# Retention in three bursts, and its read-out turned by VectorE and a trip to DRAM instead of TensorE

## The chip, the cores and the metric

The kernel runs on one core of one Trainium2 chip. The metric is the time of the device in microseconds (us) for one execution, lower is better. The engines of a core have short names in the profile: PE is TensorE's matmul, PEld its weight load, DVE is VectorE, ACT is ScalarE, POOL is GpSimd, SP is SyncE, which here only sends DMA transfers.

## The reference

A trunk of two layers on a sequence of 512 tokens and 1024 channels. Each layer normalizes its input, projects it, runs three mixers side by side (RWKV-7, retention and a spatial gating unit, SGU), merges them by sigmoid gates, projects back, and ends with a gated feed-forward part. The change touches retention (4 heads, q and k of 64, v of 128 channels, chunks of 128 tokens) and the merge:

```python
def retention_branch(p, cos, sin):
    q, k, v, g = jnp.split(p, [RET_QK_WIDTH, 2 * RET_QK_WIDTH, 2 * RET_QK_WIDTH + RET_V_WIDTH], axis=-1)
    q = rotary(q, cos, sin); k = rotary(k, cos, sin) * (RET_QK_DIM ** -0.5)
    ...
    scores = jnp.einsum('bhnid,bhnjd->bhnij', qc, kc) * decay_in[:, None]
    inner = jnp.einsum('bhnij,bhnje->bhnie', scores, vc)
    kv = jnp.einsum('bhnjd,bhnje,hj->nbhde', kc, vc, k_dec)
    _, R_prev = lax.scan(lambda R, kv_n: (R * chunk_decay + kv_n, R), zeros, kv)
    cross = jnp.einsum('bhnid,nbhde,hi->bhnie', qc, R_prev, q_dec)
    y = inner + cross
    y = y * lax.rsqrt(jnp.mean(y * y, axis=-1, keepdims=True) + EPS)
    return y.reshape(B, S, RET_V_WIDTH) * jax.nn.silu(g)
# merge: for each branch, y (512 channels) @ W_branch -> 1024 channels, times sigmoid(gate), summed over branches
```

The einsums are cut here to their core; the batch is 1.

## The kernel before

**Matrix products.** Activations lie with channels on the partitions and the 512 tokens along the free axis. Every float32 product of a weight and an activation is made of three: both are split into a high part and the rest (hi and lo of an activation, sh and sl, or wh and wl, of a weight), and PE adds lo x sh, hi x sh and hi x sl into one PSUM tile `acc` (line L153). A product over 512 channels is so 4 x 3 = 12 matmuls of 128x512; I call them by their number.

**The way of a weight.** SP loads 256 KB of raw weight into a tile `wr` (L123); there are NRAW = 3 of these. ScalarE casts it to `sh` (L136), VectorE takes the difference `sl` (L137), and with that the raw tile is free for the next load. Casts stand some products ahead of their use in the order (AHEAD, three or more). All engines run their own instructions in the order written, which a scheduler has fixed when the program is built; within it the kernel keeps some orders by hand.

**Order in the mixer.** The string SEQ sets the order of the second half of a layer's mixer: S is one call of retention (`ret_row`), H loads q and k of retention (`ret_heads`: qF, kF from DRAM, qS and vs copied to the other half of the partitions by ScalarE's queue), G is one of the four SGU pieces (`sgu_out`: 4 matmuls, then hi and lo of `sgm`), U a part of the SGU projection, Y the read-out of retention (`ret_out`), and 0, 2 and 1 are one merge each (`merge`) of RWKV, SGU and retention. Eight merges of each branch make a layer.

**Retention** runs in five calls: each reads out the chunk before (scores x v and state R x q into the tiles X), makes the scores of the next, and the first two make the states R. After a read-out ScalarE squares it by heads (`rsq`, sums in `rss`), VectorE multiplies it with the silu gate into `vt` (called yg in the code), GpSimd makes `rrr`, the inverse root of the mean, and ScalarE scales each head's 128x128 block. The result has tokens on the partitions; `ret_out` turns it with 16 PE transposes a layer (L959) and splits it from PSUM into hi and lo.

**A merge** takes a tile `gth`, which GpSimd's queue fills with the gates from DRAM (L1021), makes the 12 matmuls, and lets VectorE form (gate + 1) x product (L1024). SGU's result is added by GpSimd, retention's by VectorE (L1027), and the sum is split by ScalarE and VectorE (L145, L146) for the projection back.

Of the kernel before, what the change touches and what calls it, by code (L numbers as in the profile page):

```python
# [17 lines left out]
S = 512  # L18
NC = 4
# [2 lines left out]
RWC, RETC, SGC = 1792, 1536, 1024  # L22
NU, NR, NFP = 31, 16, 39
FILL = (35, 2, 1)
SEQ = "0 H 0 0 G G S U S U G S 0 G S 0 0 S 2 2 0 0 Y 2 2 1 2 1 2 1 2 1 2 1 1 1 1"
NRAW = 3
START = "z0 w0 z1 w1 z2 w2 z3 s0 z4 s1 w3 z5 s2 s3 w4 z6 s4 w5 z7 s5 s6 w6 s7 w7"
AHEAD = {None: 2, "p": 4, "r": 3, "f": 3, "u": 5}
# [21 lines left out]
class Emit:  # L50
# [312 lines left out]
    def mixer(self, l, nst):  # L363
        self.pool = None
        with self.tc.tile_pool(name=f"rw{l}", bufs=1) as rp:
            self.rwp = rp
            self.filler = self.fillers(l)
            st = self.rwkv(l, nst)
        self.fill(99, True)
        self.rp = self.tc.tile_pool(name=f"ff{l}", bufs=NFP)  # L370
        self.fp = self.rp.__enter__()
        self.gup = self.f(n="gup")
        with self.tc.high_priority():
            self.nc.sync.dma_start(self.gup, self.a["gup"][l])
        self.pool = "f"
        sg, out = self.sgu_v(l), self.rwkv_out(l, *st)
        self.wsp = self.split(self.ws.rearrange("p g i -> p (g i)"), self.f)
        for step in (sg, sg, out, sg, None, out, sg, out, out):
            next(step) if step else self.sgu_bias()
        yrw, ysg, mg, out, m2 = self.yrw, [], [], [], 0  # L380
        self.pool = "r"
        rest = self.sgu_u(l, range(2, 4))
        rows = iter([(None, 0), (0, 1), (1, 2), (2, 3), (3, None)])
        for step in SEQ.split():
            if step == "S":
                self.ret_row(*next(rows))
            elif step == "G":
                ysg.append(self.sgu_out(len(ysg)))
            elif step == "H":
                self.ret_heads()  # L390
            elif step == "U":
                next(rest), next(rest)
            elif step == "Y":
                yret = self.ret_out()
            elif step == "0":
                mg.append(self.merge(l, 0, len(mg), yrw))
            elif step == "2":
                mg[m2] = self.merge(l, 2, m2, ysg, mg[m2])
# [468 lines left out]
    def ret_heads(self):  # L867

        A, V, T, po = self.nc.scalar, self.nc.vector, self.nc.tensor, self.tc.keep_in_program_order
        self.qF, self.kF = [], []  # L870
        for j in range(4):
            t = self.r((128, 4, 128), n="qF" if j < 2 else "kF")
            self.nc.sync.dma_start(t.rearrange("p c t -> p (c t)"), self.qk[128 * j:128 * j + 128, :])
            (self.qF if j < 2 else self.kF).append(t)
        self.qS, Rt = self.r(n="qS"), [self.f((128, 2, 2, 128), n="R") for _ in range(4)]
        for h in range(2):
            self.nc.scalar.dma_start(self.qS[64 * h:64 * h + 64], self.qF[1][64 - 64 * h:128 - 64 * h].rearrange("p c t -> p (c t)"))
        self.Rs, vs = [None] + [Rt[n // 2][:, n % 2] for n in range(7)], [self.f((128, 2, 2, 128), n="vs") for _ in range(2)]
        self.vs = [vs[c // 2][:, c % 2] for c in range(NC)]
        for c in range(NC):  # L880
            for h in range(2):
                self.nc.scalar.dma_start(self.vs[c][64 * h:64 * h + 64], self.heads(self.vt[c], h)[64 - 64 * h:128 - 64 * h])
# [20 lines left out]
            else:  # L903
                V.tensor_tensor(self.Rs[n + 1], self.Rs[n], at(n), op=ADD)

    def ret_row(self, read, score):


        nc, V, A, T, po = self.nc, self.nc.vector, self.nc.scalar, self.nc.tensor, self.tc.keep_in_program_order
        hv = [slice(0, 64), slice(64, 128)]  # L910
        X, new = [self.sm((128, 4, 128)) for _ in range(2)], [[True, True], [True, True]]
        hd = [(j, p, h) for j in range(2) for p in range(2) for h in range(2)]

        def mm(b, q, o, lhsT, rhs, stop=True):
            po(T.matmul(o, lhsT, rhs, start=new[b][q], stop=stop, skip_group_check=True))  # L915
            new[b][q] = False

        if read is not None:
            v, g = self.vt[read], self.yg[read]
            for j, p, h in [(j, p, 1 - h) for j, p, h in hd]:  # L920
                i, o = 2 * j + h, h ^ j
                w = v[hv[p], 128 * i:128 * i + 128] if p == o else self.vs[read][hv[o], j, :]
                mm(o, p, X[o][hv[p], j, :], self.sc[hv[o], h, p, :], w, read == p == 0)
            for j, p, h in hd:
                if read or p:
                    o, ts = h ^ j, slice(128 * read + 64 * p, 128 * read + 64 * p + 64)
                    q = self.qS if j else self.qF[0].rearrange("p c t -> p (c t)")
                    mm(o, p, X[o][hv[p], j, :], q[hv[o], ts], self.Rs[2 * read + p][hv[o], j, :])
        if score is not None:
            for j, p, h in hd:  # L930
                ts = slice(64 * p, 64 * p + 64)
                mm(h, h ^ j, X[h][hv[h ^ j], 2, ts], self.kF[j][hv[h], score, ts], self.qF[j][hv[h], score, ts])
        if read is not None:
            sq, ss = self.u((128, 4, 128), n="rsq"), self.small((128, 4), "rss")
            for i in range(4):
                A.activation(sq[:, i, :], X[i % 2 ^ i // 2][:, i // 2, :], AF.Square, accum_out=ss[:, i:i + 1])
            for o in range(2):
                V.tensor_tensor(self.heads(g, o), X[o][:, 0:2, :], self.heads(g, o), op=MUL)
        if score is not None:
            sc = self.u((128, 2, 2, 64), n="sc")  # L940
            for h in range(2):
                V.tensor_tensor(sc[:, h], X[h][:, 2, :].rearrange("q (p t) -> q p t", t=64), self.c("le64").unsqueeze(1).to_broadcast([128, 2, 64]), op=MUL)
            self.sc = sc
            if score < 2:
                self.ret_states(4 * score, 4 + 3 * score)
        if read is not None:
            V.tensor_scalar(ss, ss, 4.0 / 128, 4e-6, op0=MUL, op1=ADD)
            rr = self.small((128, 4), "rrr")
            nc.gpsimd.tensor_tensor(rr, ss, self.c("mhalf")[:, 0:4], op=POW)
            for i in range(4):  # L950
                o = g[:, 128 * i:128 * i + 128]
                A.activation(o, o, AF.Copy, scale=rr[:, i:i + 1])

    def ret_out(self):
        out = []
        for h in range(4):
            pt = self.sm()
            for c in range(NC):
                self.tc.keep_in_program_order(self.nc.tensor.transpose(pt[:, c * 128:c * 128 + 128], self.yg[c][:, h * 128:h * 128 + 128], self.c("ident")))  # L959
            out.append(self.split(pt, self.f))  # L960
        return out


# [53 lines left out]
    def merge(self, l, br, m, y, sum=None, add=None):  # L1017

        nc = self.nc
        t = self.f(n="gth")  # L1020
        nc.gpsimd.dma_start(t, self.gd[br, m])  # L1021
# [279 lines left out]
```

## Time and profile before

| | |
|---|---|
| median of 3 runs | 1703.14 us (1702.77 to 1706.36) |
| the profiled execution's own time | 1702.28 us |
| its span, first to last instruction | 1700.6 us |
| mean granted TensorE clock | 0.999 |
| busy: PE, PEld | 1692.3 us (100%), 1390.6 us (82%) |
| busy: DVE, ACT, POOL | 1141.6 (67%), 765.9 (45%), 245.4 us (14%) |
| largest groups: the three matmuls of L153 with `sh` | 432.3, 431.6, 431.1 us, 1108 each |

Busy shares are of the span. A row of the timeline gives the start in us from the span's begin, the length, engine, line, operation and output<-inputs with the number of records; in brackets stands how long the engine sat idle before it and what ended that. A row of a table of groups ends in "busy us, mean ns of one | idle us of the engine before them, and what ended it". In a table of stretches each engine has its busy us, then come PE's clock, the busy share of the DMA engines and GB/s. A 128x128 float32 matmul can leave two records.

### The profile page before, as it was taken

Reading aid. Unit: us, or ns where it says so; the run is one execution under the profiler, and the core shown is the slowest. Engines: PE = TensorE matmul, PEld = TensorE weight load, DVE = VectorE, ACT = ScalarE, POOL = GpSimd, SP = SyncE. Lnnn points to the kernel's source line nnn. Section 1 sums busy time; section 2 is a strip of 40 time slices with the busy share of each in tenths; the row PEclk is TensorE's granted clock in tenths of the full one; section 3 lists DMA queues with packets and bytes.
Section 4 is the critical chain, followed back from the end, with each engine's and each line's share of the span. In section 5 each row is a group of like instructions: output and inputs, shape, how many; then the busy total and the mean of one; then the engine's idle time right before and its main releaser. Section 6 shows DMA issues by size and latency. Waiting matters only on the chain.

```text
span 1700.6 us, 28356 instructions
## 1 busy us (share of the span) xinstructions
PE 1692.3 (100%) x10564; PEld 1390.6 (82%) x10564; DVE 1141.6 (67%) x2032; ACT 765.9 (45%) x1341; POOL 245.4 (14%) x326
## 2 busy tenths in 40 slices
PE   9999999999999999999999999999999999999998
PEld 7888877888888888888888888778888888888887
DVE  7887856567569777653367786564765798876432
ACT  7564433535355444333255634345343554443322
POOL 1122235114100000000011203441141000000010
PEclk9999999999999999999999999999999999999999
DMA  5334566446443333243332346555364454432531
GB/s 175 91 101 151 147 151 152 141 130 194 137 149 100 96 97 99 69 119 110 115 113 80 112 142 155 148 141 161 108 210 141 132 138 123 124 107 68 155 100 55
DMA packets 151337, 214.20 MB, mean 126 GB/s; under 512 B 48416, under 2 KB 57248, under 8 KB 151200
## 3 DMA queue, kind: packets, MB, share of 16 engines
q1 hardware_dynamic: 129552, 171.62, 34.2%
q0 software_dynamic: 9600, 21.77, 4.9%
q10 hardware_dynamic: 12048, 19.00, 3.4%
q8 instruction: 83, 1.36, 0.3%
q14 instruction: 54, 0.44, 0.1%
HBM read 181.92 MB, written 23.07 MB: 121 GB/s over the span
## 4 chain that ended last, share of the span: by engine, by line
PE 99%; DMA 0%; ACT 0%; DVE 0%; issue 0%
PE acc L153 88%; PE sm L153 4%; PE sm L647 2%; PE acc L287 1%; PE sm L561 1%; PE sm L915 1%; PE acc L1009 0%; PE sm L524 0%; PE sm L523 0%; DMA g<-pcols 0%; PE sm L898 0%; PE sm L959 0%; PE sm L805 0%; PE sm L795 0%; PE sm L578 0%; PE sm L579 0%
## 5 line engine op out<-in xcount | busy, mean ns | idle before, releaser
L153 PE MATMUL acc<-lo,sh 128*128 128x512 f32 x1108 | 432.3, 390 | 0.0
L153 PE MATMUL acc<-hi,sh 128*128 128x512 f32 x1108 | 431.6, 390 | 0.0
L153 PE MATMUL acc<-hi,sl 128*128 128x512 f32 x1108 | 431.1, 389 | 0.0
L136 ACT CAST sh<-wr 128x512 fp32r<-128x512 f32 (+1 forms) x385 | 235.1, 615 | 380.2 <-PE acc L153 263.4
L137 DVE TENSOR_TENSOR sl<-wr,sh 128x512 fp32r<-128x512 f32 (+1 forms) x385 | 263.4, 687 | 170.5 <-ACT sh L136 104.8
L153 PEld LDWEIGHTS acc<-lo,sh 128*128 128x128 f32 x1108 | 208.0, 188 | 44.1 <-issue 0.7
L153 PEld LDWEIGHTS acc<-hi,sl 128*128 128x128 f32 x1108 | 208.0, 188 | 43.7 <-issue 0.3
L153 PEld LDWEIGHTS acc<-hi,sh 128*128 128x128 f32 x1108 | 208.0, 188 | 42.9 <-issue 0.2
L136 ACT CAST wh<-wr 128x512 fp32r<-128x512 f32 x194 | 120.2, 620 | 227.9 <-PE acc L153 209.2
L153 PE MATMUL acc<-lo,wh 128*128 128x512 f32 x556 | 219.4, 395 | 0.0
L153 PE MATMUL acc<-hi,wl 128*128 128x512 f32 x556 | 217.0, 390 | 0.0
L153 PE MATMUL acc<-hi,wh 128*128 128x512 f32 x556 | 216.6, 390 | 0.0
L137 DVE TENSOR_TENSOR wl<-wr,wh 128x512 fp32r<-128x512 f32 x195 | 138.9, 712 | 111.6 <-ACT wh L136 104.7
L153 PEld LDWEIGHTS acc<-hi,wl 128*128 128x128 f32 x556 | 104.4, 188 | 22.6 <-issue 0.7
L153 PEld LDWEIGHTS acc<-lo,wh 128*128 128x128 f32 x556 | 104.3, 188 | 22.6 <-issue 0.3
L153 PEld LDWEIGHTS acc<-hi,wh 128*128 128x128 f32 x556 | 104.4, 188 | 20.9
L153 PE MATMUL acc<-ah,sh 128*128 128x512 f32 x352 | 108.3, 389 | 0.0
L1077 DVE TENSOR_TENSOR fu<-acc,rsF 128x512 f32<-128x512 f32 x88 | 60.5, 689 | 62.3 <-PE acc L153 62.3
L1079 ACT ACTIVATE cv<-fu,pc 128x512 f32<-128x512 f32 x88 | 71.6, 816 | 50.4 <-DVE fu L1077 47.5
L153 PE MATMUL acc<-wl,hi 128*128 128x512 f32 x192 | 78.0, 406 | 0.0
L1080 DVE SCALAR_TENSOR_TENSOR cv<-fu,pc,cv 128x511 f32<-128x511 f32 x88 | 65.4, 746 | 18.6 <-ACT cv L1079 18.6
L153 PEld LDWEIGHTS acc<-ah,sh 128*128 128x128 f32 x352 | 66.1, 188 | 13.7
(335 smaller groups left out, 2450.1 us busy)
## 6 DMA issues: line engine op xcount, KB each, us to landing
wr<-wall SPq DMA_DIRECT2D x480, 256.0 KB, 2.7
gd<-gth ACTq DMA_DIRECT2D x48, 256.0 KB, 3.3
gth<-gd POOLq DMA_DIRECT2D x48, 256.0 KB, 3.3
wr<-wdt SPq DMA_DIRECT2D x44, 256.0 KB, 2.7
wr<-wdn SPq DMA_DIRECT2D x40, 256.0 KB, 2.7
x<-xT SPq DMA_DIRECT2D x8, 256.0 KB, 4.7
tn<-ysq POOLq DMA_DIRECT2D x32, 64.0 KB, 3.3
tab<-rot ACTq DMA_DIRECT2D x8, 256.0 KB, 3.9
```

What stands on the lines that cost most here:

```text
L136: self.kept((high or self.nc.scalar.copy)(hi[:, :n], raw[:, :n]))
L137: self.kept(self.nc.vector.tensor_tensor(lo[:, :n], raw[:, :n], hi[:, :n], op=SUB))
L153: i = self.nc.tensor.matmul(*x, **y, **kw)
L287: po(self.nc.tensor.matmul(pss[j], w[:, j * 128:j * 128 + 128], x, start=k == n == 0, stop=k == 7 and n == 2))
L561: i = T.matmul(pK[hv[1 - h], j, :], bk[hv[h], c, 1, :], x[hv[h], c, :], start=True, stop=True)
L647: po(T.matmul(o, l, r, start=start, stop=True, skip_group_check=True))
L915: po(T.matmul(o, lhsT, rhs, start=new[b][q], stop=stop, skip_group_check=True))
L1077: V.tensor_tensor(u, ps, self.rsF, op=MUL)
L1079: A.activation(t, u, AF.Identity, scale=self.p("cw2", j), bias=self.p("cb", j))
L1080: V.scalar_tensor_tensor(t[:, 1:], u[:, :511], self.p("cw1", j), t[:, 1:], op0=MUL, op1=ADD)
```

## The change

Retention runs in three calls instead of five: the scores of all four chunks with the first half of the states; the read-out of chunks 0 and 1 with the rest of the states; the read-out of chunks 2 and 3. The loads of qF and kF go in the order 0, 2, 1, 3. After ScalarE has scaled a block, VectorE turns it in 32x32 squares (STREAM_TRANSPOSE) into `yz`; behind the last call ScalarE's queue writes the four heads to a DRAM tile in 16 transfers of 64 KB (32x4x128, runs of 512 bytes), and SP loads each head back as a tile `yF` of 128x512, which ScalarE and VectorE split into hi and lo. SEQ changes with it: between the last call of retention and the first merge of retention now stand ten other merges, three of RWKV and seven of SGU. The gate tiles of SGU's and retention's merges come from another pool of buffers (u instead of f).

```diff
-SEQ = "0 H 0 0 G G S U S U G S 0 G S 0 0 S 2 2 0 0 Y 2 2 1 2 1 2 1 2 1 2 1 1 1 1"
+SEQ = "0 H 0 0 0 G G S U U G S 0 G S 0 0 2 2 0 2 2 2 2 Y 2 1 2 1 1 1 1 1 1 1"
 # ret_heads
-        for j in range(4):
+        for j in (0, 2, 1, 3):
 # ret_row
-    def ret_row(self, read, score):
+    def ret_row(self, read):
...
+        if read is None:
+            for c in range(NC):
+                for j, p, h in hd:
+                    ts = slice(64 * p, 64 * p + 64)
+                    mm(h, h ^ j, X[h][hv[h ^ j], c, ts], self.kF[j][hv[h], c, ts], self.qF[j][hv[h], c, ts])
+            self.ret_states(0, 4)
+            self.sc = [self.u((128, 8, 64), n="sc") for _ in range(2)]
...
+            return
+        cs = range(read, read + 2)
...
+        if read == 0:
+            self.ret_states(4, 7)
+        ss = self.small((128, 2, 4), "rss")
+        for c in cs:
+            sq, g = self.u((128, 4, 128), n="rsq"), self.yg[c]
             for i in range(4):
+                A.activation(sq[:, i, :], X[i % 2 ^ i // 2][:, 2 * (c - read) + i // 2, :], AF.Square, accum_out=ss[:, c - read, i:i + 1])
...
+        rr = self.small((128, 2, 4), "rrr")
+        nc.gpsimd.tensor_tensor(rr, ss, self.c("mhalf")[:, 0:8].rearrange("p (c i) -> p c i", i=4), op=POW)
+        if read == 0:
+            self.yd, self.yz = self.turned(), [self.u((128, 4, 4, 32), n="yz") for _ in range(4)]
+        for c in cs:
             for i in range(4):
+                o = self.yg[c][:, 128 * i:128 * i + 128]
+                A.activation(o, o, AF.Copy, scale=rr[:, c - read, i:i + 1])
+                V.transpose(self.yz[i][:, :, c, :], o.rearrange("p (b f) -> p b f", f=32))
+        for i in range(4) if read else ():
+            d = self.yd[128 * i:128 * i + 128].rearrange("(b f) (q t) -> f b q t", b=4, q=4)
+            for q in range(4):
+                nc.scalar.dma_start(d[:, :, q, :], self.yz[i][32 * q:32 * q + 32].rearrange("f b c t -> f b (c t)"))
 # ret_out
-        for h in range(4):
-            pt = self.sm()
-            for c in range(NC):
-                self.tc.keep_in_program_order(self.nc.tensor.transpose(pt[:, c * 128:c * 128 + 128], self.yg[c][:, h * 128:h * 128 + 128], self.c("ident")))
-            out.append(self.split(pt, self.f))
+        for i in range(4):
+            t = self.u(n="yF")
+            self.tc.keep_in_program_order(self.nc.sync.dma_start(t, self.yd[128 * i:128 * i + 128, :]))
+            t = t.rearrange("p (q c t) -> p c q t", q=4, c=4)
+            hi, lo = [self.f((128, 4, 4, 32), F32R, n) for n in ("hi", "lo")]
+            self.nc.scalar.copy(hi, t)
+            self.nc.vector.tensor_tensor(lo, t, hi, op=SUB)
 # merge
-        t = self.f(n="gth")
+        t = (self.u if br else self.f)(n="gth")
```

Lines behind the change shift in the new kernel: the gate load L1021 becomes L1035, VectorE's gate product L1024 becomes L1038, rrr L949 becomes L951, the squares L936 become L946, the scaling L952 becomes L957. L962 is the new write to DRAM, L972 the new split.

Three places of the new order are needed below. The numbers behind the names count tiles, so the same role has another number in the two kernels. First GpSimd, in layer 0, from the first scale factor `rrr` of a read-out to the last; before:

```order
L949 TENSOR_TENSOR rrr_4347<-rss_4319,con 128x4
L1021 DMA gth_4449<-gd_1454 128x512
L949 TENSOR_TENSOR rrr_4443<-rss_4432,con 128x4
L1021 DMA gth_4527<-gd_1496 128x512
L1021 DMA gth_4549<-gd_1538 128x512
L1021 DMA gth_4604<-gd_2000 128x512
L1021 DMA gth_4627<-gd_2146 128x512
L1021 DMA gth_4650<-gd_1580 128x512
L1021 DMA gth_4672<-gd_1622 128x512
L949 TENSOR_TENSOR rrr_4521<-rss_4510,con 128x4
```

and now:

```order
L951 TENSOR_TENSOR rrr_4458<-rss_4442,con 128x8
L1035 DMA gth_4481<-gd_1496 128x512
L1035 DMA gth_4599<-gd_1538 128x512
L1035 DMA gth_4621<-gd_1580 128x512
L1035 DMA gth_4689<-gd_1622 128x512
L1035 DMA gth_4643<-gd_2000 128x512
L1035 DMA gth_4666<-gd_2146 128x512
L1035 DMA gth_4711<-gd_2264 128x512
L1035 DMA gth_4734<-gd_2358 128x512
L1035 DMA gth_4757<-gd_2453 128x512
L1035 DMA gth_4780<-gd_2547 128x512
L951 TENSOR_TENSOR rrr_4565<-rss_4549,con 128x8
```

Six gate loads between two factors have become ten, and a factor covers two chunks. Second ScalarE, around the high part of the fourth SGU piece (`hi<-sgm`); before:

```order
L136 CAST sh_4454<-wr_4354 128x512
L952 ACTIVATE vt_3737<-vt_3737,rrr_4443 128x128 x4
L136 CAST sh_4532<-wr_4372 128x512
L136 CAST sh_4554<-wr_4452 128x512
L136 CAST sh_4609<-wr_4530 128x512
L145 CAST hi_4479<-sgm_4476 128x512
L936 ACTIVATE rsq_4509,rss_4510<-sm_4483 128x128 x2
```

and now, from the scaling of chunk 1 on:

```order
L957 ACTIVATE vt_3737<-vt_3737,rrr_4458 128x128 x4
L136 CAST sh_4604<-wr_4362 128x512
L136 CAST sh_4626<-wr_4484 128x512
L136 CAST sh_4648<-wr_4602 128x512
L136 CAST sh_4671<-wr_4624 128x512
L145 CAST hi_4511<-sgm_4508 128x512
L136 CAST sh_4694<-wr_4646 128x512
L946 ACTIVATE rsq_4550,rss_4549<-sm_4515 128x128
```

Four weights' casts now stand between the scaling and the piece, where three stood. Third ScalarE at the read-out, in which `sm` is the PSUM tile of the PE transposes; before:

```order
L952 ACTIVATE vt_3747<-vt_3747,rrr_4598 128x128 x4
L136 CAST sh_4808<-wr_4756 128x512
L136 CAST sh_4831<-wr_4779 128x512
L145 CAST hi_4699<-sm_4694 128x512
L145 CAST hi_4708<-sm_4703 128x512
L145 CAST hi_4717<-sm_4712 128x512
L145 CAST hi_4726<-sm_4721 128x512
```

and now, where `tn` is the DRAM tile:

```order
L136 CAST sh_4785<-wr_4737 128x512
L957 ACTIVATE vt_3742<-vt_3742,rrr_4565 128x128 x4
L957 ACTIVATE vt_3747<-vt_3747,rrr_4565 128x128 x4
L962 DMA tn_4460<-yz_4461 32x4x128 x4
L962 DMA tn_4460<-yz_4462 32x4x128 x4
L962 DMA tn_4460<-yz_4463 32x4x128 x4
L962 DMA tn_4460<-yz_4464 32x4x128 x4
L972 CAST hi_4805<-yF_4803 128x512
L136 CAST sh_4832<-wr_4760 128x512
L972 CAST hi_4811<-yF_4809 128x512
L136 CAST sh_4855<-wr_4783 128x512
```

The sixteen writes stand in one row between the scaling and the first head's split, and the four splits are now spread between weights' casts.

More of the change, by code (lines that the diff above doesn't have):

```diff
@@ L382, in mixer @@
         rest = self.sgu_u(l, range(2, 4))
-        rows = iter([(None, 0), (0, 1), (1, 2), (2, 3), (3, None)])
+        rows = iter([None, 0, 2])
         for step in SEQ.split():
             if step == "S":
-                self.ret_row(*next(rows))
+                self.ret_row(next(rows))
             elif step == "G":
@@ L911, in ret_row @@
         X, new = [self.sm((128, 4, 128)) for _ in range(2)], [[True, True], [True, True]]
-        hd = [(j, p, h) for j in range(2) for p in range(2) for h in range(2)]
+        hd = [(j, p, h) for j in range(2) for p in range(2) for h in (1, 0)]
         def mm(b, q, o, lhsT, rhs, stop=True):
@@ L916, in mm @@
             new[b][q] = False
-        if read is not None:
-            v, g = self.vt[read], self.yg[read]
-            for j, p, h in [(j, p, 1 - h) for j, p, h in hd]:
+        if read is None:
[5 more added lines that the diff above has]
+            self.sc = [self.u((128, 8, 64), n="sc") for _ in range(2)]
+            for h in range(2):
+                V.tensor_tensor(self.sc[h], X[h].rearrange("q c (p t) -> q (c p) t", t=64), self.c("le64").unsqueeze(1).to_broadcast([128, 8, 64]), op=MUL)
+            return
@@ L921, in ret_row @@
+        cs = range(read, read + 2)
+        for c in cs:
+            for j, p, h in hd:
                 i, o = 2 * j + h, h ^ j
-                w = v[hv[p], 128 * i:128 * i + 128] if p == o else self.vs[read][hv[o], j, :]
-                mm(o, p, X[o][hv[p], j, :], self.sc[hv[o], h, p, :], w, read == p == 0)
+                w = self.vt[c][hv[p], 128 * i:128 * i + 128] if p == o else self.vs[c][hv[o], j, :]
+                mm(o, p, X[o][hv[p], 2 * (c - read) + j, :], self.sc[h][hv[o], 2 * c + p, :], w, c == p == 0)
@@ L924, in ret_row @@
+        for c in cs:
             for j, p, h in hd:
-                if read or p:
-                    o, ts = h ^ j, slice(128 * read + 64 * p, 128 * read + 64 * p + 64)
+                if c or p:
+                    o, ts = h ^ j, slice(128 * c + 64 * p, 128 * c + 64 * p + 64)
                     q = self.qS if j else self.qF[0].rearrange("p c t -> p (c t)")
[L928 to L932, printed above, removed]
@@ L933, in ret_row @@
-        if read is not None:
-            sq, ss = self.u((128, 4, 128), n="rsq"), self.small((128, 4), "rss")
+                    mm(o, p, X[o][hv[p], 2 * (c - read) + j, :], q[hv[o], ts], self.Rs[2 * c + p][hv[o], j, :])
+        if read == 0:
+            self.ret_states(4, 7)
+        ss = self.small((128, 2, 4), "rss")
+        for c in cs:
+            sq, g = self.u((128, 4, 128), n="rsq"), self.yg[c]
             for i in range(4):
-                A.activation(sq[:, i, :], X[i % 2 ^ i // 2][:, i // 2, :], AF.Square, accum_out=ss[:, i:i + 1])
+                A.activation(sq[:, i, :], X[i % 2 ^ i // 2][:, 2 * (c - read) + i // 2, :], AF.Square, accum_out=ss[:, c - read, i:i + 1])
@@ L937, in ret_row @@
             for o in range(2):
[L938 to L949, printed above, removed]
-            for i in range(4):
-                o = g[:, 128 * i:128 * i + 128]
-                A.activation(o, o, AF.Copy, scale=rr[:, i:i + 1])
+                V.tensor_tensor(self.heads(g, o), X[o][:, 2 * (c - read):2 * (c - read) + 2, :], self.heads(g, o), op=MUL)
+        V.tensor_scalar(ss, ss, 4.0 / 128, 4e-6, op0=MUL, op1=ADD)
@@ new lines, in ret_row @@
+        rr = self.small((128, 2, 4), "rrr")
+        nc.gpsimd.tensor_tensor(rr, ss, self.c("mhalf")[:, 0:8].rearrange("p (c i) -> p c i", i=4), op=POW)
+        if read == 0:
+            self.yd, self.yz = self.turned(), [self.u((128, 4, 4, 32), n="yz") for _ in range(4)]
+        for c in cs:
+            for i in range(4):
+                o = self.yg[c][:, 128 * i:128 * i + 128]
+                A.activation(o, o, AF.Copy, scale=rr[:, c - read, i:i + 1])
+                V.transpose(self.yz[i][:, :, c, :], o.rearrange("p (b f) -> p b f", f=32))
@@ L954, in ret_out @@
+        for i in range(4) if read else ():
+            d = self.yd[128 * i:128 * i + 128].rearrange("(b f) (q t) -> f b q t", b=4, q=4)
+            for q in range(4):
+                nc.scalar.dma_start(d[:, :, q, :], self.yz[i][32 * q:32 * q + 32].rearrange("f b c t -> f b (c t)"))
     def ret_out(self):
         out = []
-        for h in range(4):
-            pt = self.sm()
-            for c in range(NC):
-                self.tc.keep_in_program_order(self.nc.tensor.transpose(pt[:, c * 128:c * 128 + 128], self.yg[c][:, h * 128:h * 128 + 128], self.c("ident")))
-            out.append(self.split(pt, self.f))
+        for i in range(4):
[5 more added lines that the diff above has]
+            self.nc.vector.tensor_tensor(lo, t, hi, op=SUB)
+            out.append([o.rearrange("p c q t -> p (c q t)") for o in (hi, lo)])
```

## The prediction

> **What bounds the kernel now.** I read the page first: busy shares, then the chain of work that ended last.
>
> ```profile
> span 1700.6 us, 28356 instructions
> PE 1692.3 (100%) x10564; PEld 1390.6 (82%) x10564; DVE 1141.6 (67%) x2032; ACT 765.9 (45%) x1341; POOL 245.4 (14%) x326
> PE 99%; DMA 0%; ACT 0%; DVE 0%; issue 0%
> ```
>
> TensorE (PE) is busy all the time and is 99% of the chain. So a matmul that goes is worth its whole time, work on another engine is worth nothing until PE waits for it, and any new wait of PE is paid in full. The question is therefore what PE's own stretch of the change costs, and whether something arrives late that was in time before. Next the timeline of PE through retention in layer 0 (start, length, line, operation, records); layer 1 has the same order, so all that follows counts twice.
>
> ```profile
> 369.56 0.39 PE L153 MATMUL acc<-hi,sl 128*128 128x512 f32 x1
> 369.88 0.47 PE L915 MATMUL sm<-qF,kF 64*64 64x64 f32 x16
> 370.16 1.07 PE L898 MATMUL sm<-vt,ro 64*64 64x128 f32 x32
> 371.16 0.50 PE L153 MATMUL acc<-lo,sh 128*128 128x512 f32 x1
> 371.50 0.40 PE L153 MATMUL acc<-hi,sh 128*128 128x512 f32 x1
> 371.74 0.40 PE L153 MATMUL acc<-hi,sl 128*128 128x512 f32 x1
> ...
> 374.83 0.32 PE L915 MATMUL sm<-vs,sc 64*64 64x128 f32 x1
> ...
> 377.02 0.50 PE L153 MATMUL acc<-lo,sh 128*128 128x512 f32 x1
> ...
> 382.89 0.32 PE L915 MATMUL sm<-vs,sc 64*64 64x128 f32 x1
> ...
> 383.82 0.46 PE L915 MATMUL sm<-qF,kF 64*64 64x64 f32 x16
> 384.22 0.50 PE L153 MATMUL acc<-lo,sh 128*128 128x512 f32 x1
> ...
> 387.11 1.05 PE L1009 MATMUL acc<-ws,sgv 128*128 128x128 f32 x8
> 387.92 0.48 PE L153 MATMUL acc<-lo,sh 128*128 128x512 f32 x1
> ...
> 389.69 0.32 PE L915 MATMUL sm<-vs,sc 64*64 64x128 f32 x1
> 390.18 0.40 PE L915 MATMUL sm<-R,qF 64*64 64x128 f32 x8
> 390.63 0.46 PE L915 MATMUL sm<-qF,kF 64*64 64x64 f32 x16
> 391.02 0.50 PE L153 MATMUL acc<-hi,sh 128*128 128x512 f32 x1
> ...
> 397.59 0.32 PE L915 MATMUL sm<-vs,sc 64*64 64x128 f32 x1
> 398.62 0.50 PE L153 MATMUL acc<-hi,sl 128*128 128x512 f32 x1
> ...
> 407.19 1.91 PE L959 MATMUL sm<-con,vt 128*128 128x128 f32 x16
> 408.85 0.48 PE L153 MATMUL acc<-lo,sh 128*128 128x512 f32 x1
> 409.17 0.39 PE L153 MATMUL acc<-hi,sh 128*128 128x512 f32 x1
> ```
>
> The ends are modelled, so I count from start to start. A 128x512 matmul takes 0.227 us (0.24 in the rows right behind a burst); a merge of twelve 2.72.
>
> **Part 1, the transposes, gone from PE.** 407.19 to 408.85 is 1.66 us, and the first large matmul behind them takes 0.32 instead of 0.23: 1.75 us a layer.
>
> **Part 2, five bursts become three.** The five bursts last 1.28 (369.88 to 371.16), 2.19, 1.33, 1.33 and 1.03 us, 7.16 together. Each also costs about 0.09 us before it (369.88 stands 0.32 behind the last large matmul) and 0.11 behind it (0.34 instead of 0.23): 5 x 0.20, together 8.2. The new bursts, by the same rows: scores 0.28 for one chunk (16 records, 369.88 to 370.16), states 1.00 for 32 records, read-out of one chunk 0.49 against the scores (389.69 to 390.18) and 0.45 against the states R. Burst 1: 4 x 0.28 + 1.00 = 2.12. Burst 2: 0.49 + 0.22 (chunk 0 reads half of R) + 0.94 + 24 records of states 0.75 = 2.40. Burst 3: 2 x 0.94 = 1.88. With 3 x 0.20 that is 7.0. Gain 1.2 us a layer. Both parts: 2.95 a layer, **5.9 us** in all.
>
> **Part 3, what now waits: the fourth SGU piece behind a weight load.** ScalarE and DMA rows of the same stretch before, and the prices:
>
> ```profile
> 388.64 3.24 POOL L1021 DMA_DIRECT2D gth<-gd  x6
> 392.90 0.62 ACT L136 CAST sh<-wr 128x512 fp32r<-128x512 f32 x1 [1.88 <-DMA wr<-wall]
> 393.43 0.62 ACT L145 CAST hi<-sgm 128x512 fp32r<-128x512 f32 x1
> 397.78 1.97 ACT L136 CAST sh<-wr 128x512 fp32r<-128x512 f32 x3 [2.70 <-DMA wr<-wall]
> 394.00:396.00 2.00, 2.00 (x11) 1.65 (x10) 1.93 (x5) 1.08 (x9) 0.00 (x0) 1.00 1.01 365
> DMA to landing us min/median/max: 2.4/3.6/5.9
> L717 POOL TENSOR_TENSOR rs<-s,con 128x8 f32<-128x8 f32 x8 | 13.3, 1665 | 58.2 <-DVE s L715 58.0
> L936 ACT ACTIVATE rsq<-sm 128x128 f32<-128x128 f32 x32 | 8.3, 270 | 0.0
> L137 DVE TENSOR_TENSOR sl<-wr,sh 128x512 fp32r<-128x512 f32 (+1 forms) x385 | 263.4, 687 | 170.5 <-ACT sh L136 104.8
> wr<-wall SPq DMA_DIRECT2D x480, 256.0 KB, 2.7
> gth<-gd POOLq DMA_DIRECT2D x48, 256.0 KB, 3.3
> ```
>
> Today POOL sends six gate loads in 3.2 us at 388.64; the DMA engines are then full (share 1.01, 365 GB/s), weight loads (the "landing" row: `wr` between 386 and 400) take up to 5.9 us instead of 2.7, and ScalarE idles twice for one (1.88, 2.70 us). PE does not notice: the fourth SGU piece is cut into hi at 393.43 and first needed in the merge that runs to the last burst, 397.3.
>
> In the new order POOL has ten gate loads in one row behind the first rrr, and ScalarE has hi of the fourth piece behind the cast of a weight (sh_4671) whose load can only go out when a DVE product frees one of the three raw buffers. I count from the start of the first merge behind burst 3:
> - Read-outs of burst 2 end at about -6.4: 1.88 + 0.2 (burst 3), 0.81 (the SGU matmuls, as 387.11 to 387.92), 2.72 (a merge), 0.75 (states).
> - Eight squares at 0.26, held between DVE's products, then DVE's mean: 3.5 us, to -2.9.
> - rrr on POOL, now 128x8 as in the L717 row: 1.67, to -1.2.
> - POOL sends the first gate load; 3.3 to land: +2.1.
> - DVE's gate product for the merge ahead of burst 3 waits for that gate; it and the weight's low part follow at 0.6 each: the raw buffer is free at 3.3, and SP sends the load.
> - Its landing is the unknown. From below 2.4, from above 5.9 plus the four more gates at 256 KB / 365 GB/s = 0.72 each: 8.8. I take 5.5, nearest to the long row: the load goes out 4.5 us after the first of ten gates (2.6 MB, 7.2 us of full engines), as today's late ones do behind six.
> - sh 0.62, hi 0.62, lo 0.69 and their gaps: 2.0 more. lo is there at 10.8.
>
> PE wants it as the tenth matmul of the third merge: 2 x 2.72 + 9 x 0.227 = 7.5. Stall 1: **3.3 us a layer** (0.2 to 6.6 by the two ends).
>
> **Part 4, the read-out's trip.** PE meets it after ten merges, at 27.2 plus 3.3.
>
> ```profile
> L1054 SPq DMA_DIRECT2D xr<-xz x32: 325/426/478, 1360.4 to 1505.2; - x32
> L882 ACTq DMA_DIRECT2D vs<-vt x16: 607/620/1732, 359.2 to 1209.9; - x16
> xr<-xz SPq DMA_DIRECT2D x32, 64.0 KB, 2.1
> yF<-tn SPq DMA_DIRECT2D x8, 256.0 KB, 4.1
> ```
>
> The last scales stand on ScalarE behind sh_4785, which with stall 1 comes at about 17.4 (its load waits for the raw buffer of three weights earlier, whose low part stands on DVE between the gate products of the first merges); eight scales end at 20. Then ScalarE issues 16 transfers. Their nearest row is xr: the same shape, 64 KB to DRAM, 0.43 each though on SP: 6.9 us; on ScalarE's own queue vs takes 0.62: 9.9. Behind them, in order, stands hi of head 0. The thirteenth transfer also waits until head 0 has been loaded back: 20 + 4 x 0.43 + 2.1 + 4.1 = 27.9, the last issue ends at 29.6, hi and lo at 31.0 against 30.5: **0.2 us** taken (0 to 2.1: with 0.62 an issue lo comes at 32.6; nothing where the load lands in 3 us). What queues behind on ScalarE are the casts for the next merges, and those have a merge of slack.
>
> **The rest, at nothing.** The 32 stream transposes on DVE (0.28 each as for the RWKV tiles) lie beside a DVE that is 67% busy. Burst 1 needs the second q and k tiles earlier; they are sent first-but-one and land some 0.7 us ahead of need, by the 4 us that a 256 KB load back from DRAM takes; a late one costs up to 0.7 a layer. Seven retention merges in a row at the end put gate product, sum and cut (about 2.4 us) on DVE per 2.72 us of PE; covered, and if not, W_out's last pieces are late. Gate tiles from another pool cost nothing themselves; they are what lets POOL send ten at once.
>
> **Sum.** -5.9 + 2 x (3.3 + 0.2) = +1.1 us on the profiled execution's 1702.28: 1703.4. The median of the runs, 1703.14, lies 0.86 above the profiled time, so **1704.2**. A measurement of this kernel can tell a difference of about 0.2%, 3.4 us, from none.
>
> [...]
>
> **Rivals.**
> - *No stall 1 (faster).* If SP's load shares the engines evenly with POOL's, or the first gate comes earlier, the load lands in 2.4 to 3.3 us, stall 1 is 0.2 to 1.1, and the gain stays: -5.9 + 2 x (0.2 to 1.1) = -5.5 to -3.7, 1697.6 to 1699.4. For it: the median landing of that stretch, 3.6. Against it: the late loads, 5.9. Chance 0.30. [...]
> - *The read-out's trip comes late (slower).* With issues on ScalarE at 0.62 us and the thirteenth waiting for head 0, stall 2 is 2.1 a layer: -5.9 + 2 x (3.3 + 2.1) = +4.9, 1708.0. It decides from 1.3 us a layer on beside stall 1. For it: the vs row. Against: the xr row, same shape. If stall 1 does not come, the trip starts 3 us sooner and this one vanishes too. Chance 0.18.
> - *PE's clock drops behind the stall (slower).* PE never idles today, so no row shows it; at half speed a merge would take 2.72 us more, and half a merge to a whole one slowed behind each stall is 1.4 to 2.7 a layer: 1704.2 + 2.7 to 5.4, 1707 to 1710. [...] Chance 0.05.
>
> **How the numbers follow.** My forecast (stall 1 of 1.1 to 4.4, small stall 2) has 0.47 and ends between 1700 and 1707. Faster by over 0.2%: the first rival, 0.30. Slower: 0.18 + 0.05 = 0.23. Same: 0.47. The range 1697.6 to 1708.5 takes in the first rival and most of the second.
>
> **What will show it.** Right: no transposes on PE; L915 and L898 in three blocks of about 2.1, 2.4 and 1.9 us; PE idle some 3 us in the third merge behind burst 3, put down to hi or lo of sgm, and ScalarE just before it waiting for a weight load; ten gate loads in one row on POOL. If PE shows no idle there, part 3 is wrong and the time is 1698. If PE idles before the first retention merge (lo of yF), part 4 was underpriced. Blocks that are longer than worked out, by waits for kF or R inside them, would make part 2 wrong.

## The result, and the profile after

The changed kernel takes **1714.24 us** (median of 6 runs, 1712.46 to 1717.01), the one before 1702.97 in the same comparisons (1702.58 to 1706.36). The ratio is 1.0064, 95% interval 1.0051 to 1.0077: slower by 11.3 us. Forecast were 1704.2 and a range to 1708.5, with 0.23 for slower. The runs of the changed kernel differ by 4.5 us among themselves, those of before, but for one, by 0.6; transfers hold 3% of the chain that ended last, where they held 0%. The profiled execution is the longest one, 1717.01 us. Of the experiments' runs further down, one of e8 took 6277.59 us and is left out.

From the page after (span, busy times, the chain by engine and by line, the gate loads):

```profile
span 1715.2 us, 28364 instructions
PE 1693.7 (99%) x10532; PEld 1390.9 (81%) x10532; DVE 1148.8 (67%) x2048; ACT 766.6 (45%) x1341; POOL 243.3 (14%) x322
PE 93%; DMA 3%; DVE 2%; issue 1%; ACT 1%; ACTq 0%; POOL 0%; SPq 0%; DVEq 0%; POOLq 0%
gth<-gd POOLq DMA_DIRECT2D x48, 256.0 KB, 4.9
```

PE's share of the chain has fallen from 99% to 93%, and a gate load takes 4.9 us to land instead of 3.3. PE's timeline, with the rows at which it idles (in brackets, with what ended it), first layer 0, then layer 1:

```profile
368.27 1.95 PE L1023 MATMUL acc<-ws,sgv 128*128 128x128 f32 x16
370.14 1.15 PE L915 MATMUL sm<-qF,kF 64*64 64x64 f32 x62
372.16 0.50 PE L153 MATMUL acc<-lo,sh 128*128 128x512 f32 x1
...
400.12 0.39 PE L153 MATMUL acc<-hi,sl 128*128 128x512 f32 x1
405.06 0.50 PE L153 MATMUL acc<-lo,sh 128*128 128x512 f32 x1 [4.55 <-DVE lo L146]
...
405.88 0.63 PE L153 MATMUL acc<-lo,sh 128*128 128x512 f32 x1
406.31 0.63 PE L153 MATMUL acc<-hi,sh 128*128 128x512 f32 x1
...
409.27 0.40 PE L153 MATMUL acc<-hi,sl 128*128 128x512 f32 x1
...
432.43 0.39 PE L153 MATMUL acc<-hi,sl 128*128 128x512 f32 x1
434.25 0.50 PE L153 MATMUL acc<-lo,sh 128*128 128x512 f32 x1 [1.42 <-DVE lo L973]
...
1254.73 0.50 PE L153 MATMUL acc<-lo,sh 128*128 128x512 f32 x1 [3.80 <-DVE lo L146]
...
1285.32 0.50 PE L153 MATMUL acc<-lo,sh 128*128 128x512 f32 x1 [2.86 <-DVE lo L973]
```

From start to start, less one pitch of 0.23, PE stands still for 4.7 and 1.6 us in layer 0 and, by the same rows of layer 1, 4.0 and 3.0: 13.3 us. L146 is the low part of the fourth SGU piece (stall 1), L973 that of a head of retention's read-out (stall 2). Behind 405.88 a matmul takes 0.43 us instead of 0.23. The table of stretches says why (the last three values of a row are PE's granted clock, the busy share of the DMA engines and GB/s; ahead of them stand the busy times of PE, PEld, DVE, ACT and POOL):

```profile
400.00:402.00 2.00, 0.51 (x3) 0.09 (x1) 0.00 (x0) 0.00 (x0) 0.00 (x0) 1.00 0.99 375
406.00:407.00 1.00, 1.00 (x4) 0.81 (x3) 0.64 (x2) 1.00 (x8) 0.00 (x0) 0.50 0.66 180
409.00:410.00 1.00, 1.00 (x6) 0.79 (x5) 1.00 (x3) 0.21 (x1) 0.49 (x1) 0.89 0.26 29
434.00:436.00 2.00, 1.75 (x8) 1.45 (x9) 0.79 (x2) 0.00 (x0) 1.13 (x1) 1.00 1.01 391
1256.00:1258.00 2.00, 2.00 (x6) 1.54 (x6) 1.59 (x5) 1.83 (x9) 0.51 (x1) 0.50 0.43 149
1288.00:1290.00 2.00, 2.00 (x7) 1.59 (x6) 2.00 (x3) 0.00 (x0) 1.54 (x1) 0.53 0.40 131
```

The clock is at 0.50 from 0.8 us behind the end of stall 1 on, for 3.4 us (405.88 to 409.27), and not behind the short stall of 1.6 us (the row from 434: 1.00). In the first 2 us of stall 1 (400 to 402) the busy share of the DMA engines is 0.99. The clock falls behind three of the four stalls (the last two rows are those of layer 1), and costs 8 x 0.2 = 1.6 us at each, 4.8 in all. So the profiled execution adds up: 2 x 2.75 us less work on PE (the bursts and transposes, below), 13.3 us of stalls and 4.8 of half speed make +12.6; the span has grown by 14.6, and the other 2.0 us, I take it small gaps, were not followed up.

Why the operands are late, by ScalarE's, GpSimd's and VectorE's timelines of layer 0, and the landing time of a weight load between 386 and 404 (of the three that SP sends there the trace holds it for one, the second), then of the four loads of yF:

```profile
389.83 1.67 POOL L951 TENSOR_TENSOR rrr<-rss,con 128x8 f32<-128x8 f32 x1 [26.88 <-DVE rss L949]
391.46 4.29 POOL L1035 DMA_DIRECT2D gth<-gd  x8
396.03 1.21 POOL L1035 DMA_DIRECT2D gth<-gd  x2 [0.28 <-PE acc L153]
395.61 0.69 DVE L1038 SCALAR_TENSOR_TENSOR gth<-gth,acc 128x512 f32<-128x512 f32 x1 [1.28 <-PE acc L153]
396.21 0.68 DVE L137 TENSOR_TENSOR sl<-wr,sh 128x512 fp32r<-128x512 f32 x1
403.06 0.62 ACT L136 CAST sh<-wr 128x512 fp32r<-128x512 f32 x1 [7.53 <-DMA wr<-wall]
403.58 0.61 ACT L145 CAST hi<-sgm 128x512 fp32r<-128x512 f32 x1
DMA to landing us min/median/max: 5.3/5.3/5.3
423.30 4.29 POOL L1035 DMA_DIRECT2D gth<-gd  x8
432.85 0.62 ACT L972 CAST hi<-yF 128x512 fp32r<-128x512 f32 x1 [6.40 <-DMA yF<-tn]
DMA to landing us min/median/max: 2.9/3.3/7.3
```

The raw buffer comes free when VectorE's sl ends, at 396.9; the cast of the weight that is loaded into it starts at 403.06, after ScalarE has waited 7.5 us for it: 6.2 us. At 423.30 GpSimd sends a **second** row of gate loads, of retention's merges, in the midst of which the load of the fourth head of the read-out takes 7.3 us instead of 3.3.

### The profile page after: what moved, and what is told of

Its sections match the earlier page's. It is cut to its first block, busy times and chain, and to the rows that moved or that the text cites. A ratio compares the mean times of both kernels' runs of the same rounds, so it can differ in the third digit from the quotient of the medians.

```text
span 1715.2 us, 28364 instructions
## 1 busy us (share of the span) xinstructions
PE 1693.7 (99%) x10532; PEld 1390.9 (81%) x10532; DVE 1148.8 (67%) x2048; ACT 766.6 (45%) x1341; POOL 243.3 (14%) x322
## 4 chain that ended last, share of the span: by engine, by line
PE 93%; DMA 3%; DVE 2%; issue 1%; ACT 1%; ACTq 0%; POOL 0%; SPq 0%; DVEq 0%; POOLq 0%
PE acc L153 83%; PE sm L153 4%; PE sm L647 2%; DMA wr<-wall 2%; PE acc L287 1%; PE sm L561 1%; DMA yF<-tn 1%; DVE sl L137 0%; DMA gth<-gd 0%; DMA tn<-yz 0%; ACT rsq L946 0%; DMA x<-xT 0%; DVE lo L146 0%; DVE gth L1038 0%; ACTq L962 0%
```

## The experiments

Theory A: both stalls are loads of 256 KB that go out just behind a row of eight to ten gate loads of the same size and come late for it. Rivals: the order on ScalarE and VectorE makes stall 1 by itself (B); the trip to DRAM is too long by itself (C); taking one late load away only shows the next (D). What was measured on the chip, in us against a kernel before of 1702.9 to 1703.0:

| run | median (lowest to highest) | ratio, 95% |
|---|---|---|
| e1 four raw buffers | 1712.24 (1708.52 to 1714.36) | 1.0041 to 1.0069 |
| e2 gates in the old pool | 1722.86 (1719.60 to 1724.20) | 1.0101 to 1.0128 |
| e3 fourth SGU piece early | 1709.17 (1705.29 to 1711.97) | 1.0024 to 1.0049 |
| e4 e2 + e3 | 1727.11 (1725.45 to 1727.88) | 1.0127 to 1.0155 |
| e5 retention's gates by SP | 1710.50 (1709.30 to 1712.61) | 1.0031 to 1.0056 |
| e6 e3 + e5 | 1705.22 (1702.81 to 1707.58) | 1.0002 to 1.0020 |
| e7 SGU's gates not loaded | 1713.89 (1712.72 to 1715.53) | 1.0049 to 1.0076 |
| e8 18 matmuls ahead of stall 1 | 1711.74 (1710.86 to 1711.97) | 1.0028 to 1.0065 |
| e9 e6, RWKV's gates by SP too | 1701.52 (1699.34 to 1703.91) | 0.9984 to 1.0002 |
| e10 e9, transposes on PE | 1702.89 (1702.54 to 1705.31) | 0.9992 to 1.0010 |
| e11 e6, half of RWKV's gates by SP | 1697.37 (1696.90 to 1698.86) | 0.9955 to 0.9980 |
| e12 e11, transposes on PE | 1701.01 (1700.82 to 1701.65) | 0.9980 to 0.9998 |

**e1: four raw buffers.** Around both stalls of layer 0 the engines keep their order; elsewhere some casts and loads of weights move.

```diff
-NRAW = 3
+NRAW = 4
```

> The changed kernel with four raw weight buffers instead of three; every engine keeps its order, only the weight loads go out one product earlier. Theory A (stall 1 is the load of one weight that goes out behind ten gate loads and lands 6.2 us later): that load now goes out ahead of the row of gates, hi and lo of the fourth SGU piece wait only for VectorE's own product, stall 1 falls from 4.7 to about 1 us a layer and the half-speed stretch behind it goes; stall 2 in front of the last yF piece (1.6 and 3.0 us) stays. Time about 1703 to 1705. Rival B (the piece is late by its place in VectorE's and ScalarE's order, not by the load): stall 1 stays above 4 us, time 1712 or more.

In the profile, PE's rows of the two layers:

```profile
401.15 0.50 PE L153 MATMUL acc<-lo,sh 128*128 128x512 f32 x1 [0.56 <-DVE lo L146]
406.84 0.50 PE L153 MATMUL acc<-lo,sh 128*128 128x512 f32 x1 [2.00 <-DVE gth L1038]
1254.54 0.57 PE L153 MATMUL acc<-lo,sh 128*128 128x512 f32 x1 [3.01 <-DVE gth L1038]
```

Stall 1 falls from 4.7 to 0.7 us, as A said and B did not. But a merge later PE waits 2.2 and 3.2 us for a PSUM tile, which VectorE's gate product frees: the next weight's load, now the one that goes out behind the ten gate loads (ScalarE waits 2.25 us for it), holds VectorE's order up. In layer 0 half of the gain is gone, in layer 1 most of it, and behind both waits a matmul takes 0.43 us (from 408.34 and from 1254.91). Stall 2 is 1.4 us in layer 0 and gone in layer 1. The time was missed by 7 us: the mechanism is right, rival D too.

**e2, e4: gates in the old pool**, alone and with the edit of e3.

```diff
-        t = (self.u if br else self.f)(n="gth")
+        t = self.f(n="gth")
```

> The changed kernel with all gate tiles from the old pool. GpSimd's first row still has ten gate loads behind the first scale factor; the second row of ten, which falls on the read-out's trip, becomes pairs between the sums. Theory A (stall 2 is the last yF load among ten gate loads, 7.3 us to land): stall 2 goes (below 0.3 us) and stall 1 stays at 4 to 5 us with its half-speed stretch: about 1714 - 4.6 - 1.6 = 1708. Rival C (the trip is too long by itself, through ScalarE's sixteen issues): stall 2 stays at 1.6 to 3.0 us, time about 1714.

> Both edits: fourth SGU piece early and gate tiles from the old pool. Theory A: no stall of over 0.5 us remains, and the gain of the change on PE (transposes and fewer bursts, 2.75 us a layer by the trace) is left: 1703.0 - 5.5 = 1697.5, faster than before by 0.3%. Rivals C or D: a stall of 1.5 us or more at the read-out or in the first merges remains, time 1701 or more.

Both times were missed badly. A's sign for stall 2 did come: GpSimd's second row has become pairs, the four loads of yF in layer 0 of e2 land in 2.8 to 3.1 us, and no wait for yF's low parts is left in either run. But PE stops elsewhere: in e4 for 4.3 us in burst 1 of each layer, for the second k tile, behind nine gate loads in a row, and in both runs before retention merges late in the layer; e4:

```profile
452.36 0.47 PE L153 MATMUL acc<-lo,sh 128*128 128x512 f32 x1 [1.94 <-DVE gth L1038]
457.26 0.47 PE L153 MATMUL acc<-lo,sh 128*128 128x512 f32 x1 [1.94 <-DVE gth L1038]
```

The scheduler wrote another order, I take it for want of tiles: in e4 VectorE takes the gate product of a merge only behind the split of the sum before, which waits for ScalarE; in the changed kernel the product stands ahead of that split. So this edit does more than spread the loads, and its time says nothing on A. e2 differs from the changed kernel in the pool alone, so it is shown that the late retention merges run without such stops only with the other pool; that this is for want of tiles is not shown.

**e3: the fourth SGU piece early.**

```diff
-SEQ = "0 H 0 0 0 G G S U U G S 0 G S 0 0 2 2 0 2 2 2 2 Y 2 1 2 1 1 1 1 1 1 1"
+SEQ = "0 H 0 0 0 G G S U U G G S 0 S 0 0 2 2 0 2 2 2 2 Y 2 1 2 1 1 1 1 1 1 1"
```

> The changed kernel with the fourth SGU piece made right behind the third, so its split stands on ScalarE ahead of the squares of the second call and behind no late cast; the gate loads fall into four ahead of the first scale factor and six behind it. Theory A: stall 1 and its half-speed stretch go (-4.7 - 1.7 a layer), stall 2 may stay (second row of ten still there, in other surroundings): 1700 to 1704. Rival D (PE only finds the next late thing, the weights' casts behind the same loads): another stall of 2 to 4 us in the same merges, time 1708 to 1714.

Stall 1 is gone in both layers. Stall 2 remains in layer 0 (1.8 us), with another of 2.2 us behind it; layer 1 has neither. And a third place appears: four of the ten gate loads now stand ahead of the first scale factor, so that seven go out in one row, and an eighth 6 us earlier, right ahead of the loads of the second q and k tile, and PE waits inside burst 1, 1.9 us in layer 0 and 3.2 in layer 1. In layer 0:

```profile
361.07 3.90 POOL L1035 DMA_DIRECT2D gth<-gd  x7
372.39 1.03 PE L915 MATMUL sm<-qF,kF 64*64 64x64 f32 x52 [1.88 <-DMA kF<-tn]
DMA to landing us min/median/max: 5.9/5.9/5.9
```

The last row is the landing of that k tile; in the changed kernel, with a row of three there, it takes 3.0 and burst 1 waits for nothing. The time was missed for this reason; it is A's mechanism at a place that I had not looked at.

**e5: retention's gates by SP**, one behind each weight load.

```diff
-        nc.gpsimd.dma_start(t, self.gd[br, m])
+        if br == 1:
+            self.tc.keep_in_program_order(nc.sync.dma_start(t, self.gd[br, m]))
+        else:
+            nc.gpsimd.dma_start(t, self.gd[br, m])
```

> The changed kernel with retention's eight gate loads sent by SP in a fixed order, one behind each weight load, instead of by GpSimd; all else in place. The first row of ten gate loads stays, the second is gone. Theory A: the last yF load is no longer among ten gate loads, stall 2 falls below 0.3 us; stall 1 and its half-speed stretch stay: about 1714.2 - 4.6 - 1.7 = 1708. Rival C (the trip is too long by itself): PE still waits 1.5 to 3 us for lo of yF, time about 1714.

Stall 2 is gone in both layers, stall 1 stays (4.7 and 4.2 us, behind both a matmul takes 0.43 us, from 405.49 and from 1254.15). Up to 430 us in layer 0 ScalarE and VectorE keep the order that they have in the changed kernel. The four loads of yF in layer 0, and the fourth head's split:

```profile
DMA to landing us min/median/max: 2.9/3.2/3.7
430.42 0.62 ACT L972 CAST hi<-yF 128x512 fp32r<-128x512 f32 x1 [3.90 <-DMA yF<-tn]
```

Against 7.3 us at most and 432.85. C is out: the same trip, with the same issues on ScalarE, is in time when the gates are not sent in a row beside it. The time is 2.5 us above the expectation.

**e6: both.**

> The last edit together with the fourth SGU piece made early. Theory A: neither stall is left, no stretch at half speed, and the time is that of before less the gain on PE, 1703.0 - 5.5 = 1697.5. Rival D (crowding only moves on to the next load): stalls of 2 us or more remain, time 1701 or more.

Stalls 1 and 2 are gone together; what is left is the third place, 2.13 and 2.54 us in burst 1 for the k tile, and behind each the states' records take 1.84 and 2.02 us, where they take 1.07 behind the 1.88 us of e3 (together about the 4 us a layer that the expectation of e9 names). With 1705.22 it is rival D that came:

```profile
373.00 1.65 PE L915 MATMUL sm<-qF,kF 64*64 64x64 f32 x50 [2.13 <-DMA kF<-tn]
1218.71 1.20 PE L915 MATMUL sm<-qF,kF 64*64 64x64 f32 x52 [2.54 <-DMA kF<-tn]
```

**e7: SGU's gates not loaded.** `nc.gpsimd.memset(t, 0.0)` in place of the load where `br == 2`.

> The changed kernel in which the gates of SGU's merges are zeroes set on GpSimd instead of loads from DRAM: of the first row's ten loads four are left. Not the whole computation: SGU's gates are left out. Theory A: the weight load of sh_4671 lands in 3 to 4 us instead of 6.2, stall 1 falls to 1 to 2.5 us and its half-speed stretch goes; stall 2 (its row keeps eight gate loads) stays. Time 1703 to 1708. Rival B (the order alone makes stall 1): it stays above 4 us.

With four gate loads in the first row, the weight loads between 386 and 404 and stall 1 of layer 0 read

```profile
DMA to landing us min/median/max: 2.5/2.6/3.1
402.06 0.51 PE L153 MATMUL acc<-lo,sh 128*128 128x512 f32 x1 [1.23 <-DVE lo L146]
430.51 0.79 PE L153 MATMUL acc<-lo,sh 128*128 128x512 f32 x1 [4.83 <-DVE lo L973]
```

instead of 5.3, 4.55 and 1.42: six gate loads less halve the weight's way, and stall 1 is 1.4 us (0.5 in layer 1). B is out. Stall 2 grows to 5.0 and 3.3 us: PE arrives at the read-out earlier, and eight gate loads still stand beside the fourth head (the slowest load of yF in layer 0 takes 5.1 us). That takes back the gain, so the time, 1713.89, missed the expectation though its first half was met.

**e8: 18 extra matmuls**, whose result is unused, ahead of the merge that holds stall 1.

> The changed kernel with 18 extra matmuls of 128x512 (4.1 us, result unused) on PE ahead of the merge that holds stall 1, so that PE works through most of that wait. If PE's half speed behind stall 1 comes from its idling, the granted clock stays at 1.00 there, stall 1 shrinks to below 1.5 us with the same end, and the time falls by about 1.6 a layer, to 1711. If the half speed comes with the full DMA engines or with anything else of that place, it stays at 0.50 for 3 us behind it and the time is 1714 or more.

PE idles 0.3 us at stall 1, and the granted clock stays at 1.00 there. But it then waits 2.3 us for a gate product, and the clock falls behind that:

```profile
407.94 0.50 PE L153 MATMUL acc<-lo,sh 128*128 128x512 f32 x1 [2.30 <-DVE gth L1042]
408.00:410.00 2.00, 2.00 (x6) 1.61 (x7) 2.00 (x5) 0.85 (x3) 1.12 (x1) 0.67 0.24 62
```

So in this run the half speed came behind 2.3 us of idling, and not at the place of stall 1. The time, 1711.74, is near the 1711 expected by luck, since its parts are others: a new wait with a spell of lower clock (0.67 from 408 to 410) in layer 0, and no stall above 0.6 us in layer 1.

**e9, e10: RWKV's gates by SP too** (`if br < 2`), with the trip and with PE's transposes.

> The kernel with the fourth SGU piece early, in which SP now sends RWKV's gate loads too, between the weights and behind the loads of q and k; only SGU's eight stay on GpSimd. Theory A, extended by the last run (where eight gate loads on GpSimd's queue stood right ahead of the loads of the second q and k tile and PE waited 4 us a layer inside burst 1): no row of loads is left ahead of a load that PE waits for; burst 1 takes 3.9 us with its SGU matmuls as in the changed kernel, there is no other stall of over 0.5 us and no half speed, and the time is 1696 to 1698.5, faster than before. Rival D: a new late load takes the place, time 1700 or more.

> The same kernel with the read-out of before: 16 PE transposes a layer from PSUM instead of VectorE's transposes and the trip to DRAM. If the trip is hidden in the kernel ahead, and the transposes cost their 1.75 us a layer, this one is 3.5 us slower than it, about 1700.5, and 2.5 us faster than before by the fewer bursts alone. Rival C (the trip costs as much as it saves even when paced): the two are equal within 1 us.

The profiled runs' mean granted clock is 0.999, as before, and no stall above 1 us is left, but the stretch of SGU matmuls and burst 1 takes 5.0 us instead of 3.89: the gates of RWKV's first merges now stand on SP behind the second q tile, whose load waits for its buffer, so the gate products are late and PE waits for a PSUM tile (e9):

```profile
369.80 1.16 PE L1023 MATMUL acc<-ws,sgv 128*128 128x128 f32 x8 [0.84 <-DVE sgm L1025]
```

They missed by 3.0 and 2.4 us, rival D once more. Rival C (equal within 1 us) did not come either: the trip is worth 1702.89 - 1701.52 = 1.4 us here.

**e11, e12: only RWKV's last four gates by SP** (`if br == 1 or br == 0 and m > 3`), so that GpSimd sends four, six and two at a time.

> The paced kernel with RWKV's first four gate loads back on GpSimd (on SP they stood behind the second q tile, whose load waits for its buffer until 365.6 us; VectorE's gate products and with them the PSUM tile of the second SGU piece came late, and the stretch with burst 1 took 5.0 us instead of 3.9). Theory A: that stretch takes 3.9 us again, one short wait for lo of yF of up to 1 us may remain, no half speed: 1701.5 - 2.2 = 1699.3, faster than before by 0.2%. Rival D (a load that PE waits for is late in another place again): 1701 or more.

> The same with the read-out of before (16 PE transposes a layer). Against the paced kernel with PE's transposes (1702.9) the shorter stretch with burst 1 gives 2.2 us: 1700.7, which is what fewer bursts are worth by themselves, 1.0 us a layer. The trip to DRAM would then be worth 1.4 us in all (1700.7 against 1699.3), of the 3.5 us that the transposes take on PE. If the fewer bursts are worth nothing, 1703.

e11 is faster than both kernels: ratio to before 0.9967 (0.9955 to 0.9980), 1697.37 us. From its page and timeline:

```profile
span 1695.9 us, 28352 instructions
PE 99%; DMA 1%; ACT 0%; DVE 0%; issue 0%; SPq 0%
394.09 3.23 POOL L1038 DMA_DIRECT2D gth<-gd  x6
419.86 1.13 POOL L1038 DMA_DIRECT2D gth<-gd  x2
```

PE has no wait over 0.5 us between its large matmuls, and the trip to DRAM is whole. It beat its expectation by 2 us, since the wait for yF that was allowed for did not come. Against it, e12 says what the parts of the change are worth once nothing stalls: the trip 1701.01 - 1697.37 = **3.6 us**, and the rest, the fewer bursts in their new order with the gates spread, 1702.93 - 1701.01 = **1.9 us**.

## Why the prediction was wrong

The forecast for the profiled execution was 1703.4 us; it took 1717.01, 13.6 more. Of these the clock makes 4.8, stall 2 4.2 (4.6 for 0.4), stall 1 2.1 (8.7 for 6.6) and the smaller saving on PE 0.4; some 2 us are the small gaps.

- **Parts 1 and 2, the work taken off PE: right.** 5.9 us were forecast. The changed kernel's own rows give 2.75 a layer: its bursts last 2.02 (370.14 to 372.16), 2.78 (384.18 to 386.96) and 1.91 us (390.81 to 392.72) for the forecast's 2.12, 2.40 and 1.88. e11 gains 5.6 in all. The transposes were forecast at 3.5 and measure 3.6; the bursts at 2.4, and measure 1.9 with what else e12 changes.
- **Part 3, stall 1: the mechanism right, two terms too small.** On the clock that starts with the merge behind burst 3 (392.72), rrr begins at -2.9 and ends at -1.2, as forecast to 0.1 us. The gate's way was taken from the page's median, 3.3 us; from 391.46 to the gate product at 395.61 it took 4.1 (e1 puts the wait of that product down to the gate load). The weight's way was taken as 5.5 and took 6.2. With VectorE's low part the buffer came free at +4.2 instead of 3.3, the low part of the piece at 12.3 instead of 10.8: 4.7 and 4.0 us a layer for 3.3. My upper end, 6.6, held it.
- **The first rival** (the load shares the engines evenly and lands within 3.3 us, chance 0.30) did not come: 6.2. The trace's packets show where the time goes. Of the load that SP sends at 396.92 no packet starts before 399.88, 3.0 us later; the 332 packets that start in between are all of GpSimd's queue. From 399.88 to 401.00, 52 packets of SP's queue start and 96 of GpSimd's. Why the first one comes so late is open.
- **Part 4, stall 2: the step that failed.** I took the trip to end with the first head, at 0.2 us, and called only ScalarE's issues a danger. The issues took 0.52 us each (15 in 7.8 us), between the 0.43 of xr and the 0.62 of vs, and the first head was in time (its split starts at 422.24, 29.5 on the clock of part 3, where 29.6 was forecast). The fourth head was late, because GpSimd sends a second row of ten gate loads as that head comes back. I had the first such row as the cause of stall 1 and did not look where GpSimd's next row would fall. That row was there to be read in the new order. It cost 1.6 and 3.0 us.
- **The clock behind a stall: the other step that failed.** It had 0.05 as a rival of its own. It came at three of four stalls, at 1.6 us each; the forecast's own stall of 3.3 us lies between those of 3.0 and 4.7 us behind which it came, so a fall of the clock belonged to the likeliest case. No row of before shows a lower clock behind a wait of PE: that it halves, and for how long, was my own assumption in that rival. The changed kernel shows 0.50 for 3.4 us behind 4.7, 4.0 and 3.0 us, and 1.00 behind 1.6; in e8 the clock falls behind a wait of 2.3 us.
- **"The rest, at nothing": right here, by a margin only.** Burst 1 did not wait in the changed kernel; with eight gate loads in place of four it waits 1.9 to 3.2 us (e3, e6). The chances put 0.23 on slower; the slower case came through two things at once, each of which I had priced alone and one at the wrong head.

## What to carry to other kernels

When an edit frees buffers or evens out an order, list every row of transfers that an otherwise idle queue will now send back to back, and see which tight load goes out beside each of them: here all three places were rows of 256 KB gate loads. A saving of a few us on the bottleneck engine was worth nothing here until those rows were spread: sending part of the gates one by one between the weights, with the fourth SGU piece made earlier, turned +11.3 into -5.6 us, and the three bursts and the trip to DRAM stayed. And a forecast stall on TensorE is to be priced with a half-speed stretch that may come behind it: here one came behind three of the four stalls, those of 3.0 us and more, and cost 1.6 us each time.

## What the runs showed of the hardware that I had not expected

A 256 KB load that SP sends just behind or among seven to ten loads of GpSimd's takes longer to land in these runs: 5.3 us for a weight and 7.3 for the fourth head in the changed kernel, 4.2 to 4.8 in e1, 5.9 in e3, 5.2 in e5. With six of them it took 2.9 to 4.7 (e11), with four 2.5 to 3.1 (e7), and the page's median for weight loads is 2.7.

TensorE's granted clock fell behind waits of PE, and not always alike. In the changed kernel it falls at 405.81, 1255.73 and 1286.45, which is 0.8 to 1.1 us after PE has gone on behind the stalls of 4.7, 4.0 and 3.0 us, and stands at 0.50 for 3.4 us each time. In layer 1 of e5 (from 1253.55) and of e7 (from 1278.22) a matmul takes 0.43 us or more from the first one behind the stall on, for 6.1 us. In these rows the length of the wait alone does not tell the cases apart: of three waits of 1.94 us for a gate product, one has matmuls of 0.43 us behind it (e4, 457.26) and two have 0.23 (e4, 452.36, and e2, 457.28). What makes the difference is not shown.
